# Eight column tiles in the first group of a decoder layer's input projection, decays spread by TensorE, products on VectorE, two attention heads ahead of the gate

## The chip, the cores and the metric

The kernel runs as one program on one core of a Trainium2 chip. The metric is the device time of one execution in microseconds; the kernel before takes 1147.04 us, the median of three runs (1146.39 to 1147.17). The engines are named as the profile names them: PE (TensorE matmuls), PEld (its weight loads), DVE (VectorE), ACT (ScalarE), POOL (GpSimd), and SP, whose queue starts most of the transfers.

## What is computed

One layer of a hybrid decoder on 256 tokens of width 2048, all in float32. Cut to what matters here:

```python
h = rms_norm(x, ln_mix_pre)
q, k, v, z, xbc, dt = split(h @ w_in)             # 8 heads of q, k, v; z: gate; xbc: x, B, C of the SSM
attn = softmax(q k^T / sqrt(128) + bias, causal) v
xbc = silu(causal_dwconv4(xbc)); dt = softplus(dt + dt_bias)
a_cs = cumsum(dt * a)                             # per head (16), in two chunks of 128 tokens
decay[l, s] = exp(a_cs[l] - a_cs[s])  for s <= l
y = (C B^T * decay) (x dt) + C state exp(a_cs) + d_skip x
ssm = group_rms_norm(y * silu(z))
x = x + rms_norm([attn, ssm] @ w_out)
x = x + rms_norm(GeGLU(dwconv3(rms_norm(x) @ w_up)) @ w_down)
```

Every large product is taken as a pair of rounded float32 parts, hi and lo: hi·hi + hi·lo + lo·hi.

## The kernel before

**Weights.** All weights come as units of 128 x 1024 (512 KB) in one fixed list. `Weights.split` (lines 57 to 61) loads a unit by SP, makes hi on ACT (L60) and lo on DVE (L61). There are four buffers each for raw, hi and lo, so a unit's split starts when PE has done the unit four places before it. `take` hands the next unit to PE, and `tick` (line 206), which follows each unit, first has the next unit split, then counts down a list of deferred functions (`defer(n, ...)` runs n units later) and issues those that are due, their PE part behind the last matmul so far. Each engine works through its instructions in a fixed order, which is settled when the kernel is built, about in the order of the program.

**A column tile** is 128 columns of `w_in`, kept transposed (features x tokens): sixteen K-tiles, each with one matmul of 512 columns (L181: hi of the weights against hi and lo of h) and one of 256 (L182: lo of the weights against hi). The two halves are added on ACT and DVE (`cols_sum`). **A row chunk** is 512 output columns for two token tiles, twelve matmuls of 512 columns for each unit (L257 to L259).

**The stages of the input projection**, 88 units in this order: the first group (8 units) with four column tiles of B and C side by side (`cols_first`; two K-tiles to a unit, with `load_x` bringing x and splitting h into hi and lo as it goes, and `load_rest` bringing the token rows `xsq` for the sums of squares on ACT, the weights of dt and small tables behind three quarters of x); 32 small matmuls for dt (`pd`, L378, L379); v as two row chunks (16 units); the eight column tiles of x (16 units), each with its convolution (`conv_mix`) at once; the gate z as two row chunks (16 units); and eight heads of q and k (32 units). After that come `w_out`, and the two FFN halves.

**The SSM's side work** is deferred into v and x: time steps and cumulated decays on small tiles; `decay_rows` (L441) turns the decays into rows, writes them to DRAM through POOL's queue and reads them back spread over all 128 partitions (four transfers of 512 KB into `rows`); `ssd_decay` (L516, four calls) subtracts on DVE (L522, 32 instructions of 128 x 128), exponentiates on ACT, and multiplies by `cbT` on POOL (L525, eight of 128 x 512). `ssd_inputs` scales x by dt, by d_skip and by the chunk decay on POOL (L533 to L538, ten of 128 x 512). `ssd_diag` and `ssd_off` are the matmuls that use them. There are eight PSUM banks: four of the pool `acc`, tag a (tiles `pa`), four of `msc`, tag m (all else).

Of the kernel before, what the change touches and what calls it, by code (L numbers as in the profile page):

```python
# [93 lines left out]
def decoder_layer(ctx, tc, x, xT, win, wdt, wout, wup, wdown, relb, vec, cols, mconv, fconv,  # L94
# [222 lines left out]
    with ExitStack() as mctx:  # L317
# [3 lines left out]
        with ExitStack() as actx:  # L321
# [23 lines left out]
            def load_rest():  # L345
                for t in range(NT):
                    nc.sync.dma_start(out=xsq[:, t, :], in_=x[0, tok(t), :])
                    nc.scalar.activation(xsq[:, t, :], xsq[:, t, :], AF.Square,
                                         accum_out=ssx[:, t:t + 1])
# [35 lines left out]
            rr = ax.tile([P, NT], F32, name="rr")  # L385
            rh = ax.tile([P, NT], F32, name="rh")
            aneg = ax.tile([P, SH], F32, name="aneg")

            def token_rms():
                nc.vector.tensor_copy(rr, mean_rsqrt(ssx, 1.0 / D))  # L390
                defer(1, along_tokens, rbc, [rr[:, t:t + 1] for t in range(NT)])
                nc.vector.tensor_scalar(rh, rr, 0.5, None, op0=ALU.mult)
                nc.vector.tensor_scalar(mch, mch, 0.5, None, op0=ALU.mult)
                nc.scalar.activation(aneg, hv[:, 1, :], AF.Exp)
                nc.vector.tensor_scalar(aneg, aneg, -1.0, None, op0=ALU.mult)


# [6 lines left out]
            acd = dr.tile([SH, S], F32, name="acd")  # L404
# [36 lines left out]
            def decay_rows():  # L441
                pat = psum("pat")
                for t in range(NT):
                    nc.tensor.transpose(pat[:SH, tok(t)], acs[:, t, :], ident)
                acr = ax.tile([SH, S], F32, name="acr")
                nc.vector.tensor_copy(acr, pat[:SH, :S])
                aux(out=acd, in_=acr)
                for g in range(SG):
                    for t in range(NT):
                        aux(out=rows[:, t, g],  # L450
                            in_=bass.AP(tensor=acd.tensor, offset=acd.offset + g * 8 * S + t * P,
                                        ap=[[0, P], [S, 8], [1, P]]))
# [63 lines left out]
            def ssd_decay(t, g):  # L516

                for b in range(2):
                    seg = rows[:, t, g, b * 4:b * 4 + 4, :]
                    for i in range(4):  # L520
                        h = g * 8 + b * 4 + i
# [438 lines left out]
```

## Time and profile before

| what | value |
|---|---|
| median of three runs | 1147.04 us |
| the profiled execution | 1146.03 us |
| its span, first to last instruction | 1144.3 us |
| mean granted clock of TensorE | 0.993 |
| PE busy | 1122.8 us (98% of the span) |
| PEld busy | 956.4 us (84%) |
| DVE busy | 793.7 us (69%) |
| ACT busy | 587.7 us (51%) |
| POOL busy | 66.2 us (6%) |

Busy shares are means over stages with different limits. Of the chain that ended last, 92% is PE. A clock of 1.00 in the rows is 2.4 GHz; its lower level is half of that. In a row of the timeline the first number is the start and the second the time for all instructions of the row; successive instructions of an engine overlap a little, so a distance from start to start is shorter than a duration.

### The profile page before, as it was taken

How to read it: one execution, taken by the hardware profiler on the slowest of the kernel's cores; microseconds unless marked ns; L12 is line 12 of the kernel's file. 1: busy time of each engine (PE TensorE's matmuls, PEld its weight loads, DVE VectorE, ACT ScalarE, POOL GpSimd, SP SyncE). 2: the span in 40 equal slices, each digit the busy share in tenths (PEclk: the TensorE clock that was granted, in tenths of full speed). 3: DMA queues.
4: the chain of work that ended last, by engine and by line, in shares of the span. 5: the costliest groups of instructions: out<-in, count | busy, mean ns of one | idle time of the engine just before them, and what ended most of it. 6: DMA issues, size and time to landing. Idle time of an engine off the chain costs nothing.

```text
span 1144.3 us, 15694 instructions
## 1 busy us (share of the span) xinstructions
PE 1122.8 (98%) x5868; PEld 956.4 (84%) x5868; DVE 793.7 (69%) x1222; ACT 587.7 (51%) x901; POOL 66.2 (6%) x57
## 2 busy tenths in 40 slices
PE   9899999999999899999999999999999999999996
PEld 7777888888888798888888888888888888888885
DVE  5679866766646878877878644447878787865563
ACT  6545544544445475555555544335555555544450
POOL 0033230000010500000000000000000000000001
PEclk9999999999999999999999999999999999999999
DMA  9576554555598265555665656655665656656562
GB/s 328 201 224 218 162 165 152 170 163 164 168 332 251 79 226 186 186 185 189 189 190 184 186 189 194 186 186 187 194 189 184 186 186 189 192 186 185 188 216 74
DMA packets 61045, 217.65 MB, mean 190 GB/s; under 512 B 7231, under 2 KB 8568, under 8 KB 60072
## 3 DMA queue, kind: packets, MB, share of 16 engines
q1 hardware_dynamic: 58264, 206.84, 56.8%
q0 software_dynamic: 1696, 8.60, 2.1%
q10 hardware_dynamic: 1008, 1.20, 0.3%
q8 instruction: 46, 0.75, 0.2%
q14 instruction: 31, 0.25, 0.1%
HBM read 214.49 MB, written 2.13 MB: 189 GB/s over the span
## 4 chain that ended last, share of the span: by engine, by line
PE 92%; DMA 3%; DVE 3%; issue 1%; SPq 0%; POOL 0%; ACT 0%; DVEq 0%; POOLq 0%; ACTq 0%
PE pa L181 35%; PE pa L182 18%; PE pa L257 8%; PE pa L259 8%; PE pa L258 8%; PE ph L259 4%; PE ph L258 4%; PE ph L257 4%; DVE wlo L61 1%; DMA raw<-in_win_dram 1%; DMA xsq<-in_x_dram 1%; PE pa L189 1%; DMA rows<-acd 1%; PE py L546 1%; DVE rows L522 1%
## 5 line engine op out<-in xcount | busy, mean ns | idle before, releaser
L61 DVE TENSOR_TENSOR wlo<-raw,whi 128x1024 fp32r<-128x1024 f32 (+1 forms) x377 | 468.3, 1243 | 265.8 <-ACT whi L60 264.6
L60 ACT CAST whi<-raw 128x1024 fp32r<-128x1024 f32 (+1 forms) x377 | 394.6, 1048 | 451.2 <-PE pa L181 170.3
L181 PE MATMUL pa<-h,whi 128*128 128x512 f32 x1376 | 483.3, 394 | 0.0
L182 PE MATMUL pa<-h,wlo 128*128 128x256 f32 x1376 | 389.8, 283 | 0.0
L181 PEld LDWEIGHTS pa<-h,whi 128*128 128x128 f32 x1376 | 258.6, 188 | 59.1
L182 PEld LDWEIGHTS pa<-h,wlo 128*128 128x128 f32 x1376 | 259.2, 188 | 0.0
L181 PE MATMUL pa<-hT,whi 128*128 128x512 f32 x416 | 150.9, 401 | 0.0
L182 PE MATMUL pa<-hT,wlo 128*128 128x256 f32 x416 | 118.3, 285 | 2.8 <-DVE wlo L61 2.8
L181 PEld LDWEIGHTS pa<-hT,whi 128*128 128x128 f32 x416 | 79.2, 190 | 17.2
L787 DVE SCALAR_TENSOR_TENSOR cfc<-cfu,fcv,cfc 128x255 f32<-128x255 f32 (+1 forms) x176 | 84.6, 481 | 4.5 <-ACT cfc L785 1.5
L182 PEld LDWEIGHTS pa<-hT,wlo 128*128 128x128 f32 x416 | 79.2, 190 | 3.2 <-DVE wlo L61 3.1
L257 PE MATMUL pa<-whi,gT 128*128 128x512 f32 x176 | 69.5, 395 | 0.0
L259 PE MATMUL pa<-whi,gT 128*128 128x512 f32 x176 | 69.5, 395 | 0.0
L258 PE MATMUL pa<-wlo,gT 128*128 128x512 f32 x176 | 69.5, 395 | 0.0
L259 PE MATMUL ph<-whi,gT 128*128 128x512 f32 x160 | 63.2, 395 | 0.0
L258 PE MATMUL ph<-wlo,gT 128*128 128x512 f32 x160 | 63.2, 395 | 0.0
L257 PE MATMUL ph<-whi,gT 128*128 128x512 f32 x160 | 63.2, 395 | 0.0
L122 POOL TENSOR_TENSOR rsy<-rsa,mhalf 128x1 f32<-128x1 f32 (+1 forms) x10 | 7.8, 779 | 798.5 <-DVE rsa L151 732.3
L785 ACT ACTIVATE cfc<-cfu,fcv 128x256 f32<-128x256 f32 x88 | 52.5, 597 | 1.4 <-DVE cfu L784 1.4
L257 PE MATMUL pa<-whi,hT 128*128 128x512 f32 x128 | 52.2, 409 | 0.0
L258 PE MATMUL pa<-wlo,hT 128*128 128x512 f32 x128 | 50.6, 395 | 0.0
L259 PE MATMUL pa<-whi,hT 128*128 128x512 f32 x128 | 50.5, 395 | 0.0
(233 smaller groups left out, 1205.1 us busy)
## 6 DMA issues: line engine op xcount, KB each, us to landing
raw<-in_wup_dram SPq DMA_DIRECT2D x176, 512.0 KB, 3.5
raw<-in_wdown_dram SPq DMA_DIRECT2D x88, 512.0 KB, 3.5
raw<-in_win_dram SPq DMA_DIRECT2D x87, 512.0 KB, 3.6
raw<-in_wout_dram SPq DMA_DIRECT2D x32, 512.0 KB, 4.0
xsq<-in_x_dram SPq DMA_DIRECT2D x2, 1024.0 KB, 9.2
rows<-acd POOLq DMA_DIRECT2D x4, 512.0 KB, 7.8
xt<-in_x_dram POOLq DMA_DIRECT2D x2, 1024.0 KB, 7.1
xr<-in_xT_dram SPq DMA_DIRECT2D x7, 256.0 KB, 7.0
```

Source lines behind the costliest of these rows:

```text
L60: nc.scalar.copy(hi[:, s], raw[:, s])
L61: nc.vector.tensor_tensor(lo[:, s], raw[:, s], f32(hi[:, s]), op=ALU.subtract)
L181: nc.tensor.matmul(ps, w[0][:, s], aT[:, k, :, :], start=(k == 0), stop=False)
L182: end[0] = nc.tensor.matmul(ps[:, :S], w[1][:, s], aT[:, k, 0, :], start=False, stop=(k == KT - 1)).ins
L189: nc.tensor.matmul(both, w[0][:, s], aT[:, k, :, tok(t)], start=(t == 0 and k == 0), stop=False)
L257: nc.tensor.matmul(ps, a, w[0][:, s], start=(first and j == 0), stop=False)
L258: nc.tensor.matmul(ps, a, w[1][:, s], start=False, stop=False)
L259: end[0] = nc.tensor.matmul(ps, b, w[0][:, s], start=False, stop=(last and j == 1)).ins
L522: nc.vector.tensor_scalar(seg[:, i, :], seg[:, i, :], nacs[:, t, h:h + 1], 0.0, op0=ALU.add, op1=ALU.min)
L546: nc.tensor.matmul(py[:, i * 64:(i + 1) * 64], rows[:, t, g, i, :], xcs[t, g][:, i * 64:(i + 1) * 64], start=True, stop=True)
L785: nc.scalar.activation(c, u, AF.Identity, scale=wv[:, 2:3], bias=wv[:, 3:4])
L787: nc.vector.scalar_tensor_tensor(c[:, sh:], u[:, :S - sh], wv[:, 2 - sh:3 - sh], c[:, sh:], op0=ALU.mult, op1=ALU.add)
```

## The change

The first group takes eight column tiles, B and C and the first half of x, one K-tile of 1024 columns to a unit, so 16 units; `pab` has all eight PSUM banks. The loads are reordered to suit: the first two K-tiles of x come singly, small tables after K-tile 5, the token rows after K-tiles 7 and 9, the token norms after 13. The x columns left (four tiles) stand behind v. The decays are no longer sent through DRAM: `decay_rows` makes hi and lo parts, turns both at once, and `ssd_decay`, now one call for every two heads, spreads a head's row over the partitions by a matmul with a repeated column of the folding table (16 matmuls of 256 columns, contraction 32), from whose PSUM output DVE subtracts. The multiplication by `cbT` (now 16 of 128 x 256) and the ten scalings of x move from POOL to DVE. Heads 0 and 1 of q and k come ahead of the gate. The number of units and of large matmuls is as before.

```diff
     def cols_first(pss, aT, after):
-        for u in range(KT // 2):
+        for k in range(KT):
             w = ws.take()
-            for j in range(2):
-                for i, ps in enumerate(pss):
-                    cols_part(ps, w, aT, u * 2 + j, j * 4 + i)
+            for i, ps in enumerate(pss):
+                cols_part(ps, w, aT, k, i)
             tick()
-            after(u)
+            after(k)
...
             starts = ws.begin(4)
-            for k in range(2):
-                load_x(k, 1)
-                ws.split(*starts[0], slice(k * 512, k * 512 + 512))
-            for u in range(1, 4):
-                load_x(2 * u, 2)
+            load_x(0, 1)
+            for c in range(2):
+                ws.split(*starts[0], chunk(c))
+            load_x(1, 1)
+            ws.split(*starts[1], slice(0, UE))
+            load_x(2, 2)
+            for u in range(2, 4):
                 ws.split(*starts[u], slice(0, UE))
-            load_x(8, 2)
+            load_x(4, 2)
-            def after(u):
-                if u < 3:
-                    load_x(10 + 2 * u, 2)
-                elif u == 3:
-                    load_rest()
-            pab = [psum("pab") for _ in range(2)] + [col_psum() for _ in range(2)]
+            def after(k):
+                if k % 2 == 0 and k < 10:
+                    load_x(6 + k, 2)
+                elif k == 5:
+                    load_small()
+                elif k in (7, 9):
+                    load_rows((k - 7) // 2)
+                elif k == 13:
+                    token_rms()
+            pab = [psum("pab") for _ in range(4)] + [col_psum() for _ in range(4)]
...
             def decay_rows():
+                both = ax.tile([P, NT, 2, SH], F32R, name="both")
+                hi, lo = both[:, :, 0, :], both[:, :, 1, :]
+                nc.vector.tensor_copy(hi, acs)
+                nc.vector.tensor_tensor(lo, acs, f32(hi), op=ALU.subtract)
+                nc.vector.tensor_copy(foldr, fold)
                 pat = psum("pat")
                 for t in range(NT):
-                    nc.tensor.transpose(pat[:SH, tok(t)], acs[:, t, :], ident)
-                acr = ax.tile([SH, S], F32, name="acr")
-                nc.vector.tensor_copy(acr, pat[:SH, :S])
-                aux(out=acd, in_=acr)
-                for g in range(SG):
-                    for t in range(NT):
-                        aux(out=rows[:, t, g],
...
+                    nc.tensor.transpose(pat[:2 * SH, tok(t)],
+                                        f32(both[:, t, :, :].rearrange("p i h -> p (i h)")), ident)
+                nc.vector.tensor_copy(acsT.rearrange("p t c -> p (t c)"), pat[:2 * SH, :S])
...
-            def ssd_decay(t, g):
...
+            def ssd_decay(h):
+                g, i = divmod(h, 8)
+                pr = psum("pdr").rearrange("p (h t c) -> p h t c", h=2, t=NT)
+                for k in range(2):
+                    nc.tensor.matmul(pr[:, k].rearrange("p t c -> p (t c)"),
+                                     foldr[:, h + k:h + k + 1].to_broadcast([2 * SH, P]),
+                                     acsT.rearrange("p t c -> p (t c)"), start=True, stop=True)
+                for k in range(2):
+                    for t in range(NT):
+                        nc.vector.tensor_scalar(rows[:, t, g, i + k, :], pr[:, k, t, :],
+                                                nacs[:, t, h + k:h + k + 1], 0.0, op0=ALU.add,
+                                                op1=ALU.min)
+                for t in range(NT):
+                    seg = rows[:, t, g, i:i + 2, :]
                     nc.scalar.activation(seg, seg, AF.Exp)
-                    nc.gpsimd.tensor_tensor(seg, seg,
-                                            cbT[:, t, g, :][:, None, :].to_broadcast([P, 4, P]),
+                defer(1, ssd_mask, g, i)
+            def ssd_mask(g, i):
+                for t in range(NT):
+                    seg = rows[:, t, g, i:i + 2, :]
+                    nc.vector.tensor_tensor(seg, seg,
+                                            cbT[:, t, g, :][:, None, :].to_broadcast([P, 2, P]),
                                             op=ALU.mult)
             def ssd_inputs(t, g):
...
-                nc.gpsimd.tensor_tensor(heads(xc), heads(xg), per_head(dts[:, t, hs]), op=ALU.mult)
-                nc.gpsimd.tensor_tensor(heads(xg), heads(xg), per_head(hv[:, 2, hs]), op=ALU.mult)
+                nc.vector.tensor_tensor(heads(xc), heads(xg), per_head(dts[:, t, hs]), op=ALU.mult)
+                nc.vector.tensor_tensor(heads(xg), heads(xg), per_head(hv[:, 2, hs]), op=ALU.mult)
...
-            for i in (2, 3, 0, 1):
+            for i in range(4):
                 cols_sum(bc[:, i, :], pab[i])
-            defer(1, token_rms)
             for i in range(4):
-                defer(4 + i, conv_mix, 8 + i, bc[:, i, :], bc[:, i, :])
-            defer(4, time_steps)
-            defer(5, decays)
+                cols_sum(xsTs[i], pab[4 + i])
+            defer(1, along_tokens, rbc, [rr[:, t:t + 1] for t in range(NT)])
+            defer(1, time_steps)
+            defer(2, decays)
+            for i in range(4):
+                defer(3 + i, conv_mix, 8 + i, bc[:, i, :], bc[:, i, :])
+            defer(8, b_and_c)
             defer(9, decay_rows)
-            defer(8, b_and_c)
-            defer(10, bias_rows)
-            for i, (t, g) in enumerate(((0, 0), (1, 0), (0, 1), (1, 1))):
-                defer(14 + i, ssd_decay, t, g)
+            for f in range(4):
+                defer(7 + 2 * f, conv_mix, f, xsTs[f], xsTs[f])
+                defer(11 + 2 * f, x_tokens, f, xsTs[f])
+            defer(14, bias_rows)
+            for h in range(0, SH, 2):
+                defer(15 + h, ssd_decay, h)
+            for t in range(NT):
+                defer(18 + t, ssd_inputs, t, 0)
+            defer(24, ssd_diag, 0, 0)
+            defer(26, ssd_diag, 1, 0)
+            defer(27, ssd_off, 0)
...
-            for f in range(8):
+            for f in range(4, 8):
...
+            for t in range(NT):
+                defer(5 + t, ssd_inputs, t, 1)
+            defer(10, ssd_diag, 0, 1)
+            defer(12, ssd_diag, 1, 1)
+            defer(13, ssd_off, 1)
...
+            for h in range(2):
+                head(h)
+            for c in range(2):
+                rows_chunk(chunk_psums(), hT, range(0, KT, 2), done=gate(c))
+            for h in range(2, H):
+                head(h)
```

On the host the weights are packed in the new order.

## Rows read from the trace of the kernel before

**Rows 1.** The page's first part: busy us (share of span) xinstructions.

```profile
PE 1122.8 (98%) x5868; PEld 956.4 (84%) x5868; DVE 793.7 (69%) x1222; ACT 587.7 (51%) x901; POOL 66.2 (6%) x57
```

**Rows 2.** Waits of PE, whole span: engine, line, releaser, total us, times, longest.

```profile
PE pd L378 <- DVE wd L352: 3.6, 1, 3.6
PE pa L182 <- DVE wlo L61: 2.8, 1, 2.8
```

**Rows 3.** Timeline of PE at the first group's end: start, us, line, op.

```profile
30.31 0.28 PE L182 MATMUL pa<-hT,wlo 128*128 128x256 f32 x1
34.14 0.42 PE L378 MATMUL pd<-hT,wd 128*32 128x256 f32 x1 [3.55 <-DVE wd L352]
...
37.03 0.28 PE L378 MATMUL pd<-hT,wd 128*32 128x256 f32 x1
...
39.12 0.62 PE L257 MATMUL pa<-whi,hT 128*128 128x512 f32 x2
```

**Rows 4.** Timeline of ACT ahead of those matmuls.

```profile
30.55 1.91 ACT L348 ACTIVATE xsq<-xsq 128x2048 f32<-128x2048 f32 x1
...
32.46 0.39 ACT L351 CAST wd<-wdr 128x256 fp32r<-128x256 f32 x1
```

**Rows 5.** Busy by stretch: PE, PEld, DVE, ACT, POOL, granted clock, DMA share, GB/s.

```profile
35.00:40.00 5.00, 5.00 (x33) 4.35 (x32) 2.62 (x4) 0.79 (x3) 0.00 (x0) 0.81 0.36 113
95.00:100.00 5.00, 5.00 (x22) 4.31 (x21) 4.09 (x3) 4.45 (x7) 4.31 (x2) 0.67 0.73 222
106.73:129.73 23.00, 23.00 (x136) 20.31 (x136) 19.64 (x32) 13.62 (x27) 0.00 (x0) 1.00 0.60 185
212.78:263.60 50.82, 50.82 (x298) 44.93 (x297) 33.96 (x67) 25.09 (x48) 0.00 (x0) 1.00 0.53 166
```

**Rows 6.** Timeline of PE in the first column tiles of x.

```profile
90.50 0.39 PE L181 MATMUL pa<-hT,whi 128*128 128x512 f32 x1
93.68 0.39 PE L182 MATMUL pa<-hT,wlo 128*128 128x256 f32 x1 [2.79 <-DVE wlo L61]
...
94.97 0.63 PE L181 MATMUL pa<-hT,whi 128*128 128x512 f32 x1
...
98.61 0.40 PE L181 MATMUL pa<-hT,whi 128*128 128x512 f32 x1
...
102.82 0.40 PE L181 MATMUL pa<-hT,whi 128*128 128x512 f32 x1
```

**Rows 7.** Timeline of DVE around that wait.

```profile
78.31 1.66 DVE L522 TENSOR_SCALAR rows<-rows,nacs 128x128 f32<-128x128 f32 x8 [2.04 <-DMA rows<-acd]
...
87.39 5.10 DVE L522 TENSOR_SCALAR rows<-rows,nacs 128x128 f32<-128x128 f32 x9
92.41 1.21 DVE L61 TENSOR_TENSOR wlo<-raw,whi 128x1024 fp32r<-128x1024 f32 x1
```

**Rows 8.** Timeline of POOL ahead of and beside rows 7.

```profile
72.74 3.59 POOL L450 DMA_DIRECT2D rows<-acd  x4 [0.39 <-issue]
...
89.84 2.56 POOL L525 TENSOR_TENSOR rows<-rows,cbT 128x512 f32<-128x512 f32 x2 [1.22 <-ACT rows L524]
```

**Rows 9.** Timeline of PE in the first units.

```profile
7.45 0.73 PE L181 MATMUL pab<-hT,whi 128*128 128x512 f32 x2 [0.41 <-ACT whi L60]
...
10.30 0.73 PE L181 MATMUL pab<-hT,whi 128*128 128x512 f32 x2 [1.16 <-ACT whi L60]
```

**Rows 10.** DVE's groups by form, 0 to 320 us: busy us, mean ns, idle before.

```profile
L61 DVE TENSOR_TENSOR wlo<-raw,whi 128x1024 fp32r<-128x1024 f32 x98 | 123.0, 1258 | 46.3 <-ACT whi L60 45.5 <-issue 0.3
L522 DVE TENSOR_SCALAR rows<-rows,nacs 128x128 f32<-128x128 f32 x32 | 11.1, 413 | 3.2 <-DMA rows<-acd 3.2
L198 DVE TENSOR_TENSOR kT<-pa,kT 128x256 f32<-128x256 f32 x16 | 6.7, 418 | 0.0
L639 DVE TENSOR_TENSOR pm<-lg,bv 128x128 f32<-128x128 f32 x8 | 2.3, 284 | 0.0
L548 DVE TENSOR_TENSOR xs<-xs,py 128x512 f32<-128x512 f32 x4 | 2.7, 686 | 3.7 <-PE py L546 3.7
```

More of the change, by code (lines that the diff above doesn't have):

```diff
@@ L343, in decoder_layer, with load_small @@
             ssx = ax.tile([P, NT], F32, name="ssx")
-            def load_rest():
-                for t in range(NT):
-                    nc.sync.dma_start(out=xsq[:, t, :], in_=x[0, tok(t), :])
-                    nc.scalar.activation(xsq[:, t, :], xsq[:, t, :], AF.Square,
-                                         accum_out=ssx[:, t:t + 1])
+            def load_small():
                 nc.sync.dma_start(out=wdr, in_=wdt)
@@ L382, in decoder_layer @@
             nc.scalar.copy(dsb, pd)
[L385 to L395, printed above, removed]
             def small(name):
@@ L514, in decoder_layer @@
             xcs = {}
-            def ssd_decay(t, g):
[L518 to L521, printed above, removed]
-                        nc.vector.tensor_scalar(seg[:, i, :], seg[:, i, :], nacs[:, t, h:h + 1],
-                                                0.0, op0=ALU.add, op1=ALU.min)
-                    nc.scalar.activation(seg, seg, AF.Exp)
-                    nc.gpsimd.tensor_tensor(seg, seg,
-                                            cbT[:, t, g, :][:, None, :].to_broadcast([P, 4, P]),
+            def ssd_decay(h):
[12 more added lines that the diff above has]
+                    seg = rows[:, t, g, i:i + 2, :]
+                    nc.scalar.activation(seg, seg, AF.Exp)
+                defer(1, ssd_mask, g, i)
[4 more added lines that the diff above has]
+                                            cbT[:, t, g, :][:, None, :].to_broadcast([P, 2, P]),
                                             op=ALU.mult)
@@ L561, in ssd_off @@
                 nc.vector.tensor_tensor(xg, xg, yo, op=ALU.add)
-            for i in (2, 3, 0, 1):
+            xsTs = [ax.tile([P, S], F32, name="xsT", tag="xsT", bufs=4) for _ in range(4)]
+            for i in range(4):
                 cols_sum(bc[:, i, :], pab[i])
-            defer(1, token_rms)
             for i in range(4):
-                defer(4 + i, conv_mix, 8 + i, bc[:, i, :], bc[:, i, :])
-            defer(4, time_steps)
-            defer(5, decays)
-            defer(9, decay_rows)
-            defer(8, b_and_c)
-            defer(10, bias_rows)
-            for i, (t, g) in enumerate(((0, 0), (1, 0), (0, 1), (1, 1))):
-                defer(14 + i, ssd_decay, t, g)
+                cols_sum(xsTs[i], pab[4 + i])
[5 more added lines that the diff above has]
+            defer(8, b_and_c)
+            defer(9, decay_rows)
+            for f in range(4):
[9 more added lines that the diff above has]
+            defer(27, ssd_off, 0)
             def v_out(c):
@@ L583, in decoder_layer @@
                 rows_chunk(chunk_psums(), hT, range(0, KT, 2), done=v_out(c))
-            for f in range(8):
+            for f in range(4, 8):
                 pa = col_psum()
                 cols_tile(pa, hT)
-                xsT = ax.tile([P, S], F32, name="xsT", tag="xsT", bufs=3)
+                xsT = ax.tile([P, S], F32, name="xsT", tag="xsT", bufs=4)
                 cols_sum(xsT, pa)
                 conv_mix(f, xsT, xsT)
-                defer(5, x_tokens, f, xsT)
-                if f % 4 == 3:
-                    g = f // 4
-                    for t in range(NT):
-                        defer(8, ssd_inputs, t, g)
-                    defer(9, ssd_diag, 0, g)
-                    defer(11, ssd_diag, 1, g)
-                    defer(12, ssd_off, g)
+                defer(4, x_tokens, f, xsT)
+            for t in range(NT):
[3 more added lines that the diff above has]
+            defer(13, ssd_off, 1)
             def gate(c):
@@ L626, in gate_out @@
                     split_scaled(mT, 8 + k, tok(t), pt[:, j, :], nw[:, k:k + 1])
-            for c in range(2):
-                rows_chunk(chunk_psums(), hT, range(0, KT, 2), done=gate(c))
             def logits(h, qT, kT):
@@ L666, in values, with head @@
                 split_evac(mT, h, slice(0, S), po[:, S - 1::-1])
-            for h in range(H):
+            def head(h):
                 pq = col_psum()
```

29 lines of the change are left out of this document (21 added, 8 removed).

## The prediction

> **What bounds the kernel now.** First the page's totals: PE is busy for 98% of the span, the next engine, DVE, for 69% [rows 1]. So time is won only where PE stands still or runs slowly, and lost where PE gets more to do or has to wait. Next the waits of PE [rows 2]: apart from the two ends and the seam to the FFN, which the change doesn't touch, there are two, the dt matmuls (`pd`) waiting for `wd`, and a column tile waiting for the lo part of its weights. The timeline around each gives its price, the granted clock behind it the rest.
>
> At the end of the first group the last matmul of B and C starts at 30.31 and the first of `pd` at 34.14 [rows 3]. The pace would have been 0.12, so 3.71 us are lost. ACT shows why: it squares the second token tile (1.91 us, late because 1 MB had to land), and only then makes the hi part of `wd` [rows 4]. After the pause the granted clock reads 0.81 over 35 to 40 us [rows 5], a mixture of its two levels, 1.2 and 2.4 GHz. From 37.03 on, the last 18 of the 32 matmuls take 39.12 - 37.03 = 2.09 us, 0.116 each; all 32 would take 3.71, and took 39.12 - 34.14 = 4.98. That is 1.27 more, and **4.98 us** in all.
>
> In the second pause the matmul after 90.50 starts at 93.68 [rows 6]. A pair of a column tile takes (102.82 - 98.61) / 12 = 0.351 at full clock, its hi matmul two thirds, 0.23, so 3.18 - 0.23 = 2.95 are lost. From 94.97 to 98.61 six pairs take 3.64 where 2.11 would do: 1.53 more (clock 0.67 over 95 to 100 [rows 5]). In all **4.48 us**. DVE is the cause: 32 subtractions for the decays took 11.1 us plus 3.2 of waiting for the DRAM round trip [rows 10], whose four transfers POOL issues from 72.74 [rows 8]. The first eight took 1.66 us (0.207 each), before POOL multiplied; nine of the later ones took 5.10 (0.57 each), with POOL multiplying from 89.84 [rows 7, 8]. At 0.207 all 32 are 6.6, so DVE lost 4.5 + 3.2 us, and the lo part behind the nine came late [rows 7].
>
> **The first group.** The work is the same, 64 pairs of matmuls more here and 64 fewer behind v. A unit still carries eight pairs, 8 x 0.351 = 2.81 us, but needs one K-tile of x in place of two: 640 KB rather than 768. At the start PE waits 0.41 for the second half of unit 0 and 1.16 for unit 1 [rows 9]. The second half now stands third in SP's queue, not fourth, and unit 1's weights have 256 KB less ahead of them, but still stand behind four loads. The saving lies between 0 and 1.57; I take the middle, 0.8, as one of two waits has its load moved ahead.
>
> The small tables and the token rows are asked for six units (17 us) or more ahead of `pd` and no longer just before it, so that pause and the slow clock after it go: 4.98. What is late next are PSUM banks. The group fills all eight, so `pd` needs the first sum done, and the two row tiles of v the fifth and sixth. Six sums at 0.42 and two weight splits at 1.26 in the same queue [rows 10] are 5.0 us, plus about 0.8 for ACT's halves. The first bank closes seven pairs (2.5 us) before the group ends, and `pd` covers 3.7 more, so 6.2 us stand against 5.8. I charge 0.3; two more splits ahead of the sums would cost 2.1 (6.2 against 8.3), and no cost at all is the other end. SP is passed by the same loads in a new order; the 2 MB of token rows come while four units are in hand, 11.2 us, and I charge nothing.
>
> **The decays.** The DRAM round trip goes with its waits, and POOL's queue keeps only the bias table. PE gets 16 matmuls of 256 columns. None with a repeated stationary column is in the trace; `pd`, with 32 columns and 256 moving, takes 0.116 apiece [rows 3], and the nearest dearer row is a 512-column matmul's share, 0.23. So 1.9 to 3.7 us, all on the path; I take **1.9**, since the length streamed is the same as `pd`'s. The transposes stay two.
>
> **DVE.** It gives up nothing and takes over 16 products of 256 and ten of 512, 16 x 0.42 + 10 x 0.69 = 13.6 us [rows 10], by the durations of L198 and L548, which have these shapes; it gains the 4.5 and 3.2 above and whatever POOL's scalings cost it. These operations hide as long as DVE is not late by more than PE has in hand. A split begins when PE has left the unit four places ahead; three units, 8.4 us, remain, less hi (1.05 on ACT) and lo (1.26): **6.1 us** of lateness are free.
>
> The tightest stretch is the eight units of the four x tiles behind v. Before, 23.00 us hold four tiles and DVE is busy for 19.64 of them [rows 5]. Added now: 16 subtractions from PSUM, 3.3 at 0.207 or 4.5 at 0.284, the duration of a PSUM-fed instruction of that size (L639); four pairs of products, 3.4; five scalings, 3.4. That is 29.7 to 30.9, against 23.0 + 8 x 0.12 = 24.0 on PE. DVE ends 5.7 to 6.9 us late, right at the 6.1. In the two heads behind, half of the 50.82 us of four heads [rows 5] is 25.4, with DVE busy for 17.0; 12 subtractions (2.5 to 3.4), six products (2.5), five scalings (3.4) and four sums of the SSM (2.8) make 28.2 to 29.1, while PE gets the diagonal and state matmuls beside its 25.4. DVE no longer falls behind by more than a few us there, and the gate stage, which has spare DVE time, takes up the rest. I charge 0.5 for a short wait; zero and 4.5 (one wait as above, with its slow clock) are the ends; no gain is possible, as PE has no other wait there to lose. In v, 16 units or 45 us of PE, DVE has 16 splits (20.2), eight convolutions at (19.64 - 8 x 1.26 - 4 x 0.42) / 4 = 1.97, the four tiles of that stretch less their splits and sums (15.8), and some 25 small instructions, counted at 0.2 (5): 41.0, close but within.
>
> The Trainium skill speaks against the subtractions from PSUM ("VectorE: DVE Perf Modes", section "Why PSUM operands drop a tier"): an fp32 operation with a scalar runs at double rate from SBUF and at single rate with an operand in PSUM. No row here has that form from PSUM. By the page's cycle table one would take an estimated 0.26 us instead of the 0.207 measured from SBUF, 0.8 us more DVE lateness in the stretch above, and the sum would change by at most that.
>
> **Heads ahead of the gate** and the scheduling of the rest add no instruction on PE. The banks and buffers are as many as before. The seam, the FFN and the tail are untouched.
>
> **The sum.** 0.8 + 4.98 + 4.48 - 1.9 - 0.3 - 0.5 = 7.6 us. The profiled execution, 1146.03, becomes 1138.4; it lies 1.0 below the median of the runs, 1147.04, so the forecast for the median is **1139.4**.
>
> **The rivals.**
>
> (a) The wait returns later: DVE passes the 6.1 us in the x tiles or heads, once, with the slow clock that followed it before: 4.5 in place of 0.5, 1143.4. For it: the tally at 5.7 to 6.9 late. Against it: products are priced at full durations though successive instructions overlap, and POOL no longer slows DVE.
>
> (b) The group's end keeps a pause: all eight banks full, 2.1 for the sums, enough beside `pd`'s own break to bring 1.3 of slow clock: 3.4 in place of 0.3, 1142.5. Against it: 6.2 us of cover. Added to (a), it gives 1146.5.
>
> (c) Slower: PE's side matmuls in units 24 to 30 wait in PE's own order for DVE, for `rows` products or for one of the four tag-m banks that DVE still holds, where before they found them ready. The spread pairs, two diagonals and a head's logits meet there with DVE at its latest. Each such wait at the price seen, 2.95 + 1.53 = 4.5: three are 13.4, 1139.4 + 13.4 - 0.5 = 1152.3. It decides from 10 us on, so from the third wait. Against it: in the whole trace before, no side matmul waits for DVE but `pd` [rows 2].
>
> (d) The change doesn't do what it says: the second pause had another cause than the decays, the lag of DVE in v, and stays, 1143.9 with the new matmuls paid. Against it: the nine slow subtractions stand directly ahead of the late lo part [rows 7].
>
> **How the numbers follow.** Forecast 0.60, (a) and (d) together 0.20, (b), alone or with (a), 0.10, (c) 0.10. A measurement of this kernel tells about 0.2% from no change, so faster is below 1144.7 and slower above 1149.3. Forecast, (b) alone and about half of (a) and (d) are faster: 0.75. The other half and (b) with (a): 0.15. (c): 0.10 slower. The range goes from 1137.0 (the whole 1.57 of the start, no charge for banks and DVE: 1137.8, and 0.8 for terms read too low) to 1146.0, which takes in (a), (b) and (d) and leaves out (c) and the doubled case.
>
> **What would show it.** Right: no wait of PE for `wd`; `pd` directly behind the group, near 52 us (30.3 + 8 x 2.81 - 0.8), at 0.116 each; clock 1.00 from there to the seam; 16 new matmuls near 0.12 apart; POOL without products; DVE over 90% busy in the x tiles. Wrong: waits of PE for lo weights (a), on v's first matmul (b), on spread, diagonal or logits matmuls (c), between about 110 and 160 us; or spread matmuls at 0.23, which take 1.9 more.

## The result, and the profile after

The changed kernel takes **1141.42 us** (median of five runs, 1141.18 to 1141.6), the kernel before in the same comparison 1147.17: a ratio of 0.9941 [0.9923, 0.9958]. (The ratio is lower than that of the two medians, 0.9950: two of the five executions of the kernel before took over 1150 us.) By the medians the gain is about 5.7 us where 7.6 was forecast; time and direction lie inside the forecast, the sum is two microseconds off. The profiled execution took 1141.18, its span is 1139.0.

The page's first part and PE's waits over the whole span (engine, line, releaser, total us, times, longest), to be held against [rows 1, 2]:

```profile
PE 1124.1 (99%) x5884; PEld 955.1 (84%) x5884; DVE 794.0 (70%) x1251; ACT 589.9 (52%) x909; POOL 33.3 (3%) x34
```

```profile
PE pxt L779 <- POOL hl L758: 2.7, 2, 2.4
PE pab L181 <- ACT whi L60: 1.3, 2, 1.1
PE idle L313 <- DVE zero L310: 1.1, 1, 1.1
PE pa L189 <- DVE h L170: 1.0, 1, 1.0
PE pa L256 <- DVE xsT L198: 0.2, 1, 0.2
```

Both pauses are gone; what is left stands at the two ends and at the seam to the FFN, but for 0.2 us at the first row chunk. The stretches with the same work as the two slow ones of [rows 5] (columns: PE, PEld, DVE, ACT, POOL, granted clock, DMA share, GB/s), `pd` with the start of v and the x tiles, read 1.00 where 0.81 and 0.67 stood:

```profile
50.00:60.00 10.00, 9.82 (x63) 8.20 (x62) 6.61 (x14) 6.02 (x14) 0.00 (x0) 1.00 0.52 158
106.00:131.00 25.00, 25.00 (x140) 20.93 (x139) 21.64 (x45) 14.16 (x26) 0.00 (x0) 1.00 0.58 183
```

PE's timeline at the start and at the group's end, against [rows 3, 9]:

```profile
4.89 0.97 PE L181 MATMUL pab<-hT,whi 128*128 128x512 f32 x3 [0.21 <-ACT whi L60]
...
9.06 1.19 PE L181 MATMUL pab<-hT,whi 128*128 128x512 f32 x4 [1.07 <-ACT whi L60]
...
51.16 0.28 PE L182 MATMUL pa<-hT,wlo 128*128 128x256 f32 x1
51.28 0.28 PE L396 MATMUL pd<-hT,wd 128*32 128x256 f32 x1
...
54.89 0.28 PE L397 MATMUL pd<-hT,wd 128*32 128x256 f32 x1
55.35 0.47 PE L256 MATMUL pa<-whi,hT 128*128 128x512 f32 x1 [0.18 <-DVE xsT L198]
```

`pd` follows the last column pair by 0.12, where 3.83 lay between them. To see where the time went, the span is cut at PE's milestones: the first matmul of `pd`, the first of v, the first of `w_out` (which reads `mT`). The 64 pairs that moved into the first group are 64 x 0.351 = 22.46 us [rows 6], taken off the first stretch of after and added to the third.

| stretch of PE | before | after, made comparable | measured change | forecast |
|---|---|---|---|---|
| span's start to `pd` | 34.14 | 51.28 - 22.46 = 28.82 | -5.32 | -3.71 - 0.8 = -4.51 |
| `pd` to v | 4.98 | 4.07 | -0.91 | -1.27 + 0.3 = -0.97 |
| v to `w_out` | 256.97 | 235.48 + 22.46 = 257.94 | **+0.97** | -4.48 + 1.9 + 0.5 = **-2.08** |
| `w_out` to the end | 848.16 | 848.20 | +0.04 | 0 |

One row is off, the third. It lost a pause of 4.48, as the waits and the clock show, and yet it is longer by 0.97; so 5.45 us came in where 2.4 was charged.

### The profile page after: what moved, and what is told of

The parts are those of the page before. It is cut to its first block, busy times and chain, and to the rows that moved or that the text cites. A ratio compares the mean times of both kernels' runs of the same rounds, so it can differ in the third digit from the quotient of the medians.

```text
span 1139.0 us, 15715 instructions
## 1 busy us (share of the span) xinstructions
PE 1124.1 (99%) x5884; PEld 955.1 (84%) x5884; DVE 794.0 (70%) x1251; ACT 589.9 (52%) x909; POOL 33.3 (3%) x34
## 4 chain that ended last, share of the span: by engine, by line
PE 96%; DVE 2%; DMA 0%; issue 0%; ACT 0%; SPq 0%; POOL 0%; DVEq 0%; ACTq 0%; POOLq 0%
PE pa L181 36%; PE pa L182 18%; PE pa L256 9%; PE pa L258 8%; PE pa L257 8%; PE ph L256 4%; PE ph L257 4%; PE ph L258 4%; PE pab L181 1%; DVE wlo L61 1%; PE pa L189 1%; PE py L565 1%; PE pab L182 1%; DMA raw<-in_win_dram 0%; PE pa L192 0%
## 5 line engine op out<-in xcount | busy, mean ns | idle before, releaser
L181 PE MATMUL pa<-h,whi 128*128 128x512 f32 x1376 | 483.3, 394 | 0.0
L182 PE MATMUL pa<-h,wlo 128*128 128x256 f32 x1376 | 389.2, 283 | 0.0
L181 PEld LDWEIGHTS pa<-h,whi 128*128 128x128 f32 x1376 | 258.4, 188 | 59.6
L182 PEld LDWEIGHTS pa<-h,wlo 128*128 128x128 f32 x1376 | 258.7, 188 | 0.0
L181 PE MATMUL pa<-hT,whi 128*128 128x512 f32 x384 | 138.5, 399 | 0.0
L182 PE MATMUL pa<-hT,wlo 128*128 128x256 f32 x384 | 108.2, 283 | 0.0
L181 PEld LDWEIGHTS pa<-hT,whi 128*128 128x128 f32 x384 | 72.1, 188 | 16.6 <-issue 0.2
L182 PEld LDWEIGHTS pa<-hT,wlo 128*128 128x128 f32 x384 | 72.1, 188 | 0.3 <-issue 0.2
L256 PE MATMUL pa<-whi,mT 128*128 128x512 f32 x112 | 43.9, 392 | 0.0
```

The source lines that it names most:

```text
L181: nc.tensor.matmul(ps, w[0][:, s], aT[:, k, :, :], start=(k == 0), stop=False)
L182: end[0] = nc.tensor.matmul(ps[:, :S], w[1][:, s], aT[:, k, 0, :], start=False, stop=(k == KT - 1)).ins
L256: nc.tensor.matmul(ps, a, w[0][:, s], start=(first and j == 0), stop=False)
```

## Experiments

Since the seam adds a spread of its own (below), each kernel is given with two numbers: its time, and the stretch from v to `w_out` out of its trace, with 22.46 added where the first group has 16 units. The stretch was read once for each run, from one profiled execution. A ratio goes by executions of the kernel before taken beside that kernel, whose medians lie between 1147.03 and 1148.48, so it is not the quotient of two medians of this table.

| kernel | decays | products, scalings | median us | ratio to before | v to `w_out` |
|---|---|---|---|---|---|
| before | DRAM | POOL | 1147.17 | 1 | 256.97 |
| before_products_on_dve | DRAM | DVE | 1143.62 | 0.9966 [0.9954, 0.9977] | 252.38 |
| before_new_decays | TensorE, 32 rows | DVE | 1146.89 | 0.9993 [0.9983, 1.0002] | 257.13 |
| before_tables_first | DRAM | POOL | 1146.74 | 0.9994 [0.9984, 1.0004] | 260.02 |
| after | TensorE, 32 rows | DVE | 1141.42 | 0.9941 [0.9923, 0.9958] | 257.94 |
| after_old_decays | DRAM | POOL | 1143.22 | 0.9966 [0.9953, 0.9979] | 258.76 |
| after_dram_dve | DRAM | DVE | **1137.08** | **0.9910** [0.9896, 0.9923] | 253.39 |
| products_on_pool | TensorE, 32 rows | POOL | 1141.36 | 0.9938 [0.9923, 0.9953] | 257.96 |
| gate_first | as after | DVE | 1141.26 | 0.9936 [0.9922, 0.9951] | 258.01 |
| spread_plain | as after, column written out | DVE | 1141.76 | 0.9942 [0.9926, 0.9959] | 257.84 |
| spread_128rows | TensorE, 128 rows | DVE | 1137.94 | 0.9908 [0.9893, 0.9923] | 254.82 |
| spread_128rows_b (the same, another chip) | TensorE, 128 rows | DVE | 1139.39 | 0.9931 [0.9917, 0.9945] | 254.83 |

### What a spread pair costs

PE's timeline of after around one pair (start, us):

```profile
114.55 0.39 PE L181 MATMUL pa<-hT,whi 128*128 128x512 f32 x1
114.78 0.28 PE L182 MATMUL pa<-hT,wlo 128*128 128x256 f32 x1
114.98 0.49 PE L528 MATMUL pdr<-acsT,foldr 32*128 32x256 f32 x2
115.41 0.50 PE L181 MATMUL pa<-hT,whi 128*128 128x512 f32 x1
115.75 0.28 PE L182 MATMUL pa<-hT,wlo 128*128 128x256 f32 x1
```

From the L182 ahead to the L182 behind are 0.97 us. Without the pair these would be 0.35 (114.55 to 114.78 is 0.23, and 0.12 for an L182), so a pair costs **0.62**, eight pairs 5.0. Of it 0.43 lies between the pair's start and the next matmul's; 0.19 is lost by the neighbours: the L182 ahead has 0.20 for 0.12, the L181 behind 0.34 for 0.23. The weight loads of the same moment show where:

```profile
114.55 0.19 PEld L182 LDWEIGHTS pa<-hT,wlo 128*128 128x128 f32 x1
114.98 0.29 PEld L528 LDWEIGHTS pdr<-acsT,foldr 32*128 32x128 f32 x2 [0.24 <-issue]
115.41 0.19 PEld L181 LDWEIGHTS pa<-hT,whi 128*128 128x128 f32 x1
```

The column tile's load for the L182 of 114.78 starts at 114.55, one matmul ahead. The pair's first load and that of the L181 behind it start only at 114.98 and 115.41, with their own matmul. Two things set this pair apart from its neighbours: its contraction of 32 rows, and a stationary operand that is one column repeated. Two kernels take away one each.

**spread_128rows** pads with rows of zeros to 128:

```diff
-            acsT = ax.tile([2 * SH, NT, P], F32R, name="acsT")
-            foldr = ax.tile([2 * SH, SH], F32R, name="foldr")
+            acsT = ax.tile([P, NT, P], F32R, name="acsT")
+            foldr = ax.tile([P, SH], F32R, name="foldr")
+            nc.vector.tensor_copy(acsT.rearrange("p t c -> p (t c)"), zero)
+            nc.vector.tensor_copy(foldr, zero[:, :SH])
...
-                                     foldr[:, h + k:h + k + 1].to_broadcast([2 * SH, P]),
+                                     foldr[:, h + k:h + k + 1].to_broadcast([P, P]),
```

> The changed kernel with the folding column and the decay rows padded by zeros to 128 rows, so that the 16 spread matmuls contract over 128 rows in place of 32; the repeated stationary column stays. Theory: with 32 rows PE doesn't load the stationary operand ahead, so a spread pair costs 0.62 us with what it does to its neighbours (8 pairs, 5.0 us, in place of the forecast's 1.9). Padded, a pair should take about 0.24 and its neighbours their usual 0.12 and 0.23, 3.0 us less: 1138.4. Rival: the repeated column is to blame, or the time was lost elsewhere: unchanged, 1141.4.

The same pair in its timeline of PE, and the loads beside it:

```profile
114.09 0.28 PE L182 MATMUL pa<-hT,wlo 128*128 128x256 f32 x1
114.21 0.39 PE L530 MATMUL pdr<-acsT,foldr 128*128 128x256 f32 x2
114.44 0.39 PE L181 MATMUL pa<-hT,whi 128*128 128x512 f32 x1
114.67 0.28 PE L182 MATMUL pa<-hT,wlo 128*128 128x256 f32 x1
```

```profile
114.09 0.30 PEld L530 LDWEIGHTS pdr<-acsT,foldr 128*128 128x128 f32 x2
114.33 0.19 PEld L181 LDWEIGHTS pa<-hT,whi 128*128 128x128 f32 x1
```

Now 0.58 lies between the two L182, 0.23 for the pair, and the loads run ahead again. Eight pairs should save 8 x (0.62 - 0.23) = 3.1 us; the stretch from v to `w_out` is 3.12 shorter.

**spread_plain** keeps the 32 rows and has POOL write the column out as a plain 32 x 128 operand ahead of time:

```diff
+            def spread(h):
+                fx[h] = ax.tile([2 * SH, 2, P], F32R, name="fx", tag="wdr", bufs=1)
+                nc.gpsimd.tensor_copy(fx[h], f32(foldr[:, h:h + 2])[:, :, None].to_broadcast([2 * SH, 2, P]))
...
-                                     foldr[:, h + k:h + k + 1].to_broadcast([2 * SH, P]),
+                                     fx[h][:, k, :],
```

> The changed kernel with the stationary operand written out (128 equal columns for each head, copied by POOL two units ahead), 32 rows as before. Theory (rows are to blame): spread matmuls still 0.2 us apart, 1141.4 within 0.5. Rival (the repeated column is to blame): 0.12 apart, 1138.4.

Nothing moved: 1141.76, and PE's timeline still has 0.21 ahead of the pair, 0.43 for it and 0.34 behind:

```profile
114.68 0.28 PE L182 MATMUL pa<-hT,wlo 128*128 128x256 f32 x1
114.89 0.49 PE L534 MATMUL pdr<-acsT,fx 32*128 32x256 f32 x2
115.32 0.50 PE L181 MATMUL pa<-hT,whi 128*128 128x512 f32 x1
115.66 0.27 PE L182 MATMUL pa<-hT,wlo 128*128 128x256 f32 x1
```

So the number of rows in the contraction is the cause, not the repeated column. Why a load doesn't run ahead where the number of rows changes, no run here shows. **spread_128rows_b** ran the padded kernel once more, beside after_dram_dve:

> The kernel with 128 rows again, beside the one above on the same chip: 1138.0 within 0.5 if the executions of the kernel before agree with earlier ones; the spread matmuls 0.12 apart.

The stretch from v to `w_out` came out the same to 0.01; the median is 1.45 higher, outside the 0.5 that was expected. The difference lies behind the mixer: from the FFN's first matmul to the second half's first, 252.26 us against 251.02. The granted clock over 380 to 390 us was 0.66 in this run,

```profile
380.00:390.00 10.00, 7.13 (x35) 6.90 (x36) 9.16 (x15) 3.62 (x11) 4.54 (x3) 0.66 0.49 152
```

and 0.83 in spread_128rows:

```profile
380.00:390.00 10.00, 7.00 (x46) 6.77 (x46) 9.67 (x16) 4.75 (x13) 4.68 (x3) 0.83 0.47 152
```

What makes the clock come back later at the seam was not tried. It is why the stretch stands beside the median.

### Which part removed the second pause

**before_products_on_dve** is the kernel before with four statements moved, the decays still through DRAM:

```diff
-                    nc.gpsimd.tensor_tensor(seg, seg,
+                    nc.vector.tensor_tensor(seg, seg,
...
-                nc.gpsimd.tensor_tensor(heads(xc), heads(xg), per_head(dts[:, t, hs]), op=ALU.mult)
-                nc.gpsimd.tensor_tensor(heads(xg), heads(xg), per_head(hv[:, 2, hs]), op=ALU.mult)
+                nc.vector.tensor_tensor(heads(xc), heads(xg), per_head(dts[:, t, hs]), op=ALU.mult)
+                nc.vector.tensor_tensor(heads(xg), heads(xg), per_head(hv[:, 2, hs]), op=ALU.mult)
...
-                    nc.gpsimd.tensor_tensor(heads(xd), heads(xc), per_head(dec[:, hs]),
+                    nc.vector.tensor_tensor(heads(xd), heads(xc), per_head(dec[:, hs]),
```

> The kernel before with the products and scalings on DVE in place of POOL; the decays still go through DRAM. It tells what makes the second pause. If it is the wait for the transfers, with DVE's order fixed, the wait of PE for wlo stays at 2 us or more, and the time as before or more by DVE's extra 13.6 us where these are not hidden. If it is POOL slowing DVE, the wait goes: 4 us or more below the kernel before.

The one wait of PE in its input projection behind the first units, and its group of subtractions on DVE (busy us, mean ns, idle before), against [rows 2, 10]:

```profile
PE pd L378 <- DVE wd L352: 3.5, 1, 3.5
```

```profile
L522 DVE TENSOR_SCALAR rows<-rows,nacs 128x128 f32<-128x128 f32 x32 | 7.0, 279 | 3.4 <-DMA rows<-acd 3.4
```

No wait for `wlo` is left, though DVE still waits 3.4 us for the transfers; the closest lo part is ready 2.1 us ahead of PE. The mean went from 413 to 279 ns, and the stretch is 4.59 shorter, the price of the second pause (4.48) within 0.1. The pause was made by POOL's slowing of DVE; the DRAM round trip was hidden. The mean of 413 hides two kinds of subtraction, as the least, the middle and the longest duration in the trace of before tell (in ns):

```profile
L522 DVE TENSOR_SCALAR rows<-rows,nacs x32: 273/275/1421, 78.3 to 94.5; 128x128 f32<-128x128 f32 x32
```

Twenty-eight take 0.27 to 0.29 us and four 1.32 to 1.42, and these four lie beside a product of POOL for nearly all their time. A weight split in the same stretch, at 81.29, took 2.32 us instead of 1.2, also beside a product.

**before_new_decays** has both parts, the spread on TensorE and the products on DVE, in the old order of tiles:

```diff
-                aux(out=acd, in_=acr)
...
+                pr = psum("pdr").rearrange("p (h t c) -> p h t c", h=2, t=NT)
+                for k in range(2):
+                    nc.tensor.matmul(pr[:, k].rearrange("p t c -> p (t c)"),
+                                     foldr[:, h + k:h + k + 1].to_broadcast([2 * SH, P]),
+                                     acsT.rearrange("p t c -> p (t c)"), start=True, stop=True)
...
-                    nc.gpsimd.tensor_tensor(seg, seg,
+                    nc.vector.tensor_tensor(seg, seg,
```

> The kernel before with the new decays alone (spread by TensorE over 32 rows, products and scalings on DVE; old first group, old order). Theory: the second pause and its slow clock go (4.48 us), the 16 spread matmuls cost 5.0: the same time as before within 1 us. Rival (the second pause has another cause): a wait for wlo of 2 us or more stays in the trace, and it is 4 us or more slower.

The pause is gone here too and the time is that of before: 4.75 us longer than with the products on DVE alone. What the pause gave, the 32-row pairs took.

**after_old_decays** puts both parts back into the changed kernel: DRAM, and products on POOL.

```diff
-            def ssd_decay(h):
+            def ssd_decay(t, g):
...
-                    nc.vector.tensor_tensor(seg, seg,
-                                            cbT[:, t, g, :][:, None, :].to_broadcast([P, 2, P]),
+                    nc.gpsimd.tensor_tensor(seg, seg,
+                                            cbT[:, t, g, :][:, None, :].to_broadcast([P, 4, P]),
```

> The changed kernel with the old decays (sent through DRAM, products and scalings on POOL) in the new first group and order. Theory: the spread matmuls' 5.0 us go, a wait for wlo as in the second pause comes back (4.48): 1140.9. Rival: in the new order DVE has enough in hand to wait for the transfers, no wait of PE: 1136.4.

A wait comes back, but at another place, and 1143.22 is 2.3 above what was expected. PE's longest wait in the input projection, DVE's group of subtractions, and a stretch (columns as in [rows 5]):

```profile
PE px L492 <- DVE xsT L469: 3.3, 1, 3.3
```

```profile
L527 DVE TENSOR_SCALAR rows<-rows,nacs 128x128 f32<-128x128 f32 x32 | 14.4, 528 | 0.4 <-DMA rows<-acd 0.4
```

```profile
125.00:130.00 5.00, 2.96 (x11) 2.61 (x12) 4.86 (x10) 3.16 (x5) 0.00 (x0) 0.75 0.48 161
```

DVE waited 0.4 us for the transfers and yet the subtractions took 14.4, so DVE was late (a lo part was ready only 0.05 us ahead of PE at 115.3), and a transpose of x waited for it, with slow clock behind. A side matmul that waits in PE's order for DVE is what rival (c) described; it appears here once.

**after_dram_dve** is the changed kernel with the decays back through DRAM and the products left on DVE:

```diff
-                pr = psum("pdr").rearrange("p (h t c) -> p h t c", h=2, t=NT)
...
+                aux(out=acd, in_=acr)
...
+                        nc.vector.tensor_scalar(seg[:, i, :], seg[:, i, :], nacs[:, t, h:h + 1],
+                                                0.0, op0=ALU.add, op1=ALU.min)
```

> The changed kernel with the decays sent through DRAM as before the change, but the products and scalings on DVE. Theory: POOL beside subtractions from SBUF made the second pause, not the transfers, so without POOL's products no wait for lo weights comes back, and the spread matmuls' 5.0 us are saved: 1136.4, some 1.5 us below the kernel with 128 rows, whose spread matmuls still cost 1.9. Rival: the transfers, 2.1 MB and some 10 us of latency, come too late for the planned order of DVE: a wait of PE of 2 us or more, 1139 or above.

Its waits of PE for DVE that after doesn't have (the second one is in unit 0, at 7.0 us), and DVE's subtractions:

```profile
PE px L492 <- DVE xsT L469: 0.3, 1, 0.3
PE pa L182 <- DVE wlo L61: 0.2, 1, 0.2
```

```profile
L527 DVE TENSOR_SCALAR rows<-rows,nacs 128x128 f32<-128x128 f32 x32 | 7.0, 277 | 0.9 <-DMA rows<-acd 0.9
```

At 1137.08, 0.7 above what was expected, this beats both kernels. The stretch is 4.55 shorter than after's: TensorE's spread with 32 rows cost the changed kernel 4.6 us net and brought nothing that DVE's products alone did not.

### Where the products stand, and the order of the heads

**products_on_pool** takes back the products and scalings alone; the decays stay on TensorE.

```diff
-                    nc.vector.tensor_tensor(seg, seg,
+                    nc.gpsimd.tensor_tensor(seg, seg,
```

(and the same in the three scalings)

> The changed kernel with the products with the mask and the scalings of x on POOL, as before the change. If DVE has time in hand (lo weights were ready 5.9 us or more ahead of PE in v, x and heads), it makes no difference: 1141.4 within 0.7. If the move of the products is what removed the second pause, DVE is slowed by POOL again, lo weights come late and PE waits: 3 us or more, 1144.5 or above.

```profile
L533 DVE TENSOR_SCALAR rows<-pdr,nacs 128x128 f32<-128x128 f32 x32 | 10.1, 343 | 4.1 <-PE pdr L528 4.0
```

That is DVE's group of subtractions: 343 ns with POOL multiplying, 346 without (after). No difference in time either. Read together with the runs above, POOL slows DVE's subtractions only where they read SBUF: here 15 of the 32 lie beside a product of POOL, and these too take 0.33 to 0.35 us. What POOL does slow here are weight splits, which read SBUF: four in the input projection take 1.42 to 1.91 us instead of 1.2, and as their lo parts are still ready 6 us ahead of PE, no wait follows. So the spread alone, in the new order, leaves no second pause either: one of the two parts is enough. For the subtractions the Trainium skill ("SBUF — State Buffer", section "Who interferes with whom") has the rule: a DVE instruction with at most one SBUF input outside its two-port modes doesn't meet POOL, a scalar operation in such a mode does. The four means (413 and 528 ns from SBUF beside POOL, 277 to 279 without; 343 and 346 from PSUM) agree.

**gate_first** puts the gate ahead of all heads again, and the weights with it:

```diff
-            for h in range(2):
-                head(h)
...
-            for h in range(2, H):
+            for h in range(H):
                 head(h)
```

> The changed kernel with the gate ahead of all eight heads, as before the change. If the two heads only reorder work that PE does anyway, it makes no difference: 1141.4 within 0.7. If they cover side work of DVE that the gate would have to wait for, PE waits in the gate: 2 us or more, 1143.5 or above.

1141.26: no difference, and no wait of PE in the gate (one of 0.2 us for a lo part stands in unit 0, at 7.0 us). The two heads bring nothing.

### Whether the order of the loads would have done for the first pause

**before_tables_first** asks for `wd` and the tables ahead of the token rows, and leaves the group at four tiles:

```diff
             def load_rest():
-                for t in range(NT):
-                    nc.sync.dma_start(out=xsq[:, t, :], in_=x[0, tok(t), :])
-                    nc.scalar.activation(xsq[:, t, :], xsq[:, t, :], AF.Square,
-                                         accum_out=ssx[:, t:t + 1])
                 nc.sync.dma_start(out=wdr, in_=wdt)
...
+                for t in range(NT):
+                    nc.sync.dma_start(out=xsq[:, t, :], in_=x[0, tok(t), :])
+                    ...
```

> The kernel before, with the small tables asked for and wd split ahead of the token rows instead of behind them, and nothing else. Theory: the pause ahead of pd and its slow clock, 4.98 us by rows 3, come from this order alone: PE no longer waits for wd, and the time is 4.5 to 5.0 us below that of the kernel before. Rival: the eight tiles of the first group are needed to cover the loads; a wait for wd of over 2 us stays, and less than 2.5 us are gained.

`pd` starts at 30.02 instead of 34.14, and v 3.82 earlier, but the time is unchanged: the stretch from v to `w_out` is 3.05 longer, and the seam to the FFN takes 1.2 more in this execution. PE's waits, and ACT's timeline ahead of them:

```profile
PE pa L182 <- DVE wlo L61: 3.7, 2, 3.1
...
PE pa L257 <- ACT whi L60: 1.5, 1, 1.5
PE pa L258 <- DVE wlo L61: 1.5, 1, 1.5
```

```profile
32.31 1.92 ACT L354 ACTIVATE xsq<-xsq 128x2048 f32<-128x2048 f32 x1
...
34.21 1.04 ACT L60 CAST whi<-raw 128x1024 fp32r<-128x1024 f32 x1
```

The squares now stand behind `wd` but ahead of the splits of v's units, so v waits: 1.5 us on its first matmul, at 35.30, and 1.5 on a lo part behind it. The 3.7 of the first row is the second pause, 2.8 before, with a wait of 0.7 ahead of it. `wd` was only the first to feel that the token rows land at the group's end. In after, where the same loads have 22 us more of column tiles ahead of `pd`, neither of v's waits is left. My theory, that the order alone gives the gain, fell, and the rival's wait for `wd` isn't there either; the longer group is part of it. The longer group with the old order of loads was not run.

## Why the prediction was right, and where it was off

**First pause, right in cause and size.** 3.71 and the slow clock went; 0.12 lies ahead of `pd`, its 32 matmuls are 0.116 apart, and the clock holds. The forecast named the order of the loads and the length of the group together. The order is not enough by itself (before_tables_first); whether the length is, was not tried.

**Start, under-sized.** 1.61 us came in against 0.8, just above the upper end of 1.57. That end counted listed waits, and they hardly changed: 0.41 and 1.16 before, 0.21 and 1.07 after. But units 0 and 1, 5.62 us at the full pace, took 8.85 before (4.70 to 13.55) and 7.08 after (4.89 to 11.97), so 3.23 and 1.46 us over. Some of this is not the change. In before the first matmuls of 512 columns last as long as those at the lower clock in [rows 6], and in after they don't:

```profile
5.72 0.61 PE L181 MATMUL pa<-hT,whi 128*128 128x512 f32 x1
```

That differs by the execution: products_on_pool, with the new group, begins as slowly as the kernel before, and before_tables_first, with the old one, at the full pace. Yet unit 2 starts between 11.7 and 12.7 us in all eight runs with the new group and between 13.1 and 13.8 in the four with the old one, so the first matmuls' pace doesn't decide it. Over these runs the group ends 1.5 us earlier on average, and single ones lie up to 0.6 us from their group's mean. The distance from one unit's first matmul to the next one's would have been the right bound.

**PSUM banks, right.** v's first matmul stands 0.46 behind the last of `pd`, 0.34 more than the pace of 0.12, with 0.18 of waiting for a sum. The charge was 0.3, so rival (b) is out.

**Second pause, right in engine, wrong in the share of its parts.** The forecast gave DVE 4.5 us back from POOL and 3.2 from the DRAM wait, and counted on both. before_products_on_dve shows that the first alone is enough. Each of the two is more than the 2.95 that PE waited, so by the forecast's own numbers one part would do, and the spread on TensorE stood there as a cost without a return. Rival (d) is out, as the pause did come from the decays.

**Spread matmuls, the step that failed.** 1.9 was taken and 3.7 was the bound; 5.0 came, 0.62 a pair. The prediction's own sign of being wrong, spread matmuls at 0.23, came in (0.22 and 0.20 in the pair), and its price for that, 1.9 more, was too low, since the neighbours lose time as well. The reason given, "since the length streamed is the same as `pd`'s", looked at the moving side alone. `pd` has 128 rows, and the bound was drawn from 128-row rows as well. The trace of before held more. It does have a repeated stationary column, against what the prediction says: the two 128-row matmuls `prb` (L158) at 44.70, of 128 columns each, take 0.14 us together, though the matmul behind them has 0.31 where 0.23 is usual. And it has 32 rows between 128-row matmuls, the four `pdt` of the time steps in v, with 16 columns each:

```profile
50.27 0.40 PE L259 MATMUL pa<-whi,hT 128*128 128x512 f32 x1
50.59 0.61 PE L410 MATMUL pdt<-cst,dsb 32*128 32x16 f32 x4
51.14 0.50 PE L257 MATMUL pa<-whi,hT 128*128 128x512 f32 x1
51.47 0.40 PE L258 MATMUL pa<-wlo,hT 128*128 128x512 f32 x1
```

The matmul ahead of the four has 0.32 and the one behind 0.33, again for 0.23: the neighbours' 0.2 could have been read there. The Trainium skill ("TensorE: Matmul & The Clock Gate", section "Why this matters for your kernels") says that one matmul with 32 rows takes the time of one with 128. In this stream it doesn't: a pair costs 0.62 against 0.23. In the section "The mechanism" the Trainium skill says that a weight load overlaps running matmuls only where its group of rows differs. The trace of after disagrees: up to `w_out`, a load between two 128-row matmuls starts 0.22 us ahead of its own matmul in the median, while all nine loads at a change from 128 to 32 rows, and all nine at a change back, start with their own matmul.

**DVE in the x tiles, wrong tally, harmless.** 5.7 to 6.9 us of lateness against 6.1 free were forecast, and a charge of 0.5. There is no such wait. The tally had all side work for the eight units done inside them; DVE's timeline shows it stretched out instead, single subtractions between the steps of a convolution, and a split not behind them all:

```profile
127.23 0.34 DVE L533 TENSOR_SCALAR rows<-pdr,nacs 128x128 f32<-128x128 f32 x1
127.49 0.48 DVE L467 SCALAR_TENSOR_TENSOR cmc<-xsT,mch,cmc 128x254 f32<-128x254 f32 x1
127.88 1.23 DVE L61 TENSOR_TENSOR wlo<-raw,whi 128x1024 fp32r<-128x1024 f32 x1
129.02 0.48 DVE L467 SCALAR_TENSOR_TENSOR cmc<-xsT,mch,cmc 128x253 f32<-128x253 f32 x1
```

Of the 32 subtractions 12 start between 106 and 131 us, where the tally had 16; the last one starts at 155.6, two dozen us behind the x tiles, and DVE is busy for 21.64 of the 25.0 us from 106 to 131: 87%, not over 90. Unit by unit, the lo part was ready at least 5.9 us before PE's first use of it in v, the x tiles and the heads; in before the smallest distance was 0.05, at 93.7 us. Rival (a) is out, and (c) for this kernel.

**The price of a subtraction from PSUM.** Four in a row stand in DVE's timeline:

```profile
154.85 1.12 DVE L533 TENSOR_SCALAR rows<-pdr,nacs 128x128 f32<-128x128 f32 x4
```

The last of them takes its 0.345 whole, so they start (1.12 - 0.345) / 3 = 0.26 apart. From SBUF the prediction took 0.207, the time of eight divided by eight [rows 7]; read from start to start like these it is 0.20. 0.26 is the estimate that the prediction made from the Trainium skill's page "VectorE: DVE Perf Modes" ("Why PSUM operands drop a tier"): the trace agrees. It hangs on nothing else, since DVE had room.

**The sum again.** Against the forecast for the profiled execution, 1138.4, the measured 1141.18 is 2.8 more: 3.1 for the pairs, 0.5 for the rest of v to `w_out` (in after_dram_dve, without pairs, an excess of 0.9 is left over the 252.5 that before would take without its pause, 0.3 of it a wait; what the rest is was not found), 0.4 around the span (2.15 where 1.78 was) and 0.1 in the two other stretches, less 0.8 at the start and the 0.5 charged for DVE. The median then lay 0.2 above the profiled execution, not 1.0, which makes 2.0 for the medians. That the forecast came so near is in part luck: the 1.3 us of the start and of DVE, and the 0.8 of the median, happened to lie the other way.

## What to carry over

A change with several parts wants each priced against the same pause by itself: here either part, the products on DVE or the spread, was enough against the pause, but the spread with 32 rows spent as much again on PE, and together they looked like no gain. Small matmuls on a path bound by PE should have the contraction of their neighbours, if need be with rows of zeros, and their price is read from the distance between the neighbours on both sides, not from their own duration. Where a wait goes by reordering alone, ask what was waiting behind it for the same late data.

## What the runs showed of the hardware that I had not expected

- Where the number of rows changes between neighbouring matmuls, the weight load starts with its own matmul and not ahead of it, on the way to 32 rows and on the way back: a pair costs 0.62 us against 0.23 with 128 rows, and the way in which the stationary column is laid out doesn't matter (0.43 between the pair's start and the next matmul's, repeated or written out).
- Beside POOL's products a few of DVE's fp32 subtractions out of SBUF took 1.3 to 1.4 us instead of 0.28 (four of 32 in before, seven in after_old_decays), and weight splits up to 2.3 instead of 1.2; subtractions out of PSUM stayed at 0.33 to 0.35. So the slower-looking operand was the safer one beside POOL.
- After the seam to the FFN the granted clock came back at different times for one and the same kernel (0.83 or 0.66 over 380 to 390 us), worth 1.2 us of time between the same two matmuls.
